# DeltaNet's row products and their transposes on 128 rows instead of 6, x loaded in two parts around the first weights, and new hand-written orders on all engines

## The chip, the cores and the metric

The kernel runs on one core of a Trainium2 chip. The metric is device time in microseconds (us); the kernel before was timed at a median of 1327.37 us over three runs (1327.2 to 1327.58). Engines are named as in the profile: PE (TensorE matmuls), PEld (its weight loads), DVE (VectorE), ACT (ScalarE), POOL (GpSimd), SP (the queue that issues most DMAs).

## The reference

A trunk of two layers over 512 tokens of width 1024. Layer 0 mixes tokens by a gated DeltaNet in both directions (8 heads of 128), layer 1 by gated linear attention (GLA, 4 heads); each is followed by a squared-ReLU MLP of width 4096, with a LayerNorm after every residual. Cut to what the change touches:

```python
proj = jnp.matmul(h, w_in).astype(F32)
qkv = jax.nn.silu(_depthwise_conv(proj[..., :A_CONV_CH], conv_w.astype(F32)))
beta = sigmoid(ba[:, :, 0]); g = -exp(a_log) * softplus(ba[:, :, 1] + dt_bias)
# per direction and head, chunks of 64 tokens:
gc = jnp.cumsum(g, axis=-1)
decay_mat = jnp.exp(jnp.where(causal, gc[..., :, None] - gc[..., None, :], -jnp.inf))
a_mat = jnp.where(strict, einsum(kb, k) * decay_mat, 0.0)
sol = triangular_solve(a_mat + I, [v * beta, kb * exp(gc)])
# then the scan over chunks with qk * decay_mat, q * exp(gc), k * exp(gc_last - gc)
```

## The kernel before

Tokens stand in four tiles of 128 (x0 to x3). The program has four stages: DeltaNet (about 0 to 400 us), MLP, GLA, MLP. Products in float32 are split into a high and a low half (`wh`, `wl` of the weights, `xth`, `xtl` of the activations), and each product is three matmuls (lines 145, 147, 148: high by high, low by high, high by low). ACT makes the high halves (line 116 for weights, 219 for x), DVE the low ones (lines 117 and 220).

**The head.** `load_x` issues four DMAs for x0 to x3, each 512 KB. PE starts with `idle` matmuls (line 824) on a zeroed tile `pz`, whose result nobody reads, and then transposes each x tile, 8 blocks of 128x128 (line 207, `tp`), with `idle` matmuls between. ACT and DVE split the transposed blocks. `load_x` returns the last such split on ACT as a mark; the weights of the gates (`bst`, split into `ws`) and the first head's key weights (`k0`) are written behind that mark. The first two products, `bap` (the gates' inputs, lines 166 and 167) and `pjk` (the keys of head 0), run in halves of 256 tokens: `bap` half 0, `pjk` half 0, `bap` half 1, `pjk` half 1.

**The gates and the first head.** From `bap`, line 1472 makes `gtp`; DVE computes the log decays in a long chain (lines 1481 to 1499, tiles `gy`, `gd`, `ge`, `gl`) and PE their sums over a chunk (`gcp`). In between stand the projections of head 0 (`pjk`, `pjq`, `pjv`, `pjz`), the convolution over time (ACT line 1612 the middle tap, DVE line 1616 four more), and Silu (lines 1643 and 1647, with a table load ahead). PE then transposes keys and queries (`ktp`, line 1664).

**The row products.** In `rows`, DVE writes a row factor in three bfloat16 pieces for two directions, 6 columns (`rsp`, lines 1683 to 1687). PE transposes them per token tile (line 1690, `rtp`: 128x6 to 6x128, four per head), ACT copies the result (`rt`, 6x512, line 1692), and in `solve` a product of the selecting matrix `sel` (6x128) with `rt` spreads a row over all 128 partitions (line 1730, `ep`: contraction over 6 rows, 512 columns, two per head). A second matmul (line 1743, `mi` by `idb`) adds a mask into the same bank. `sel` is made on POOL at the start (lines 1426 to 1431). Behind `ep` stand the solve's float16 products (`hp`, `xp`, `lv`, `nw`) and the scan's float32 ones (`m`, `op`). Each of the 8 heads does this once.

**Order.** The order on every engine is written out by hand: `ORDER` holds, for each engine, its instructions' numbers in the order in which they are to run, and `written_order` chains them. Waits across engines are added by data. Filler on PE for the solve's waits is the projections of the next head, matmul by matmul.

Of the kernel before, what the change touches and what calls it, by code (L numbers as in the profile page):

```python
# [17 lines left out]
P = 128  # L18
# [796 lines left out]
def load_x(c, x, tags, zero):  # L815
    c.new_xt()
    c.new_x()
    for t in range(NT):
        c.dma(c.xt[t], x[t * P:(t + 1) * P, :])
    idle = c.bank([P, S], F32, name="idle", tag="pj")  # L820

    def warm(n=1):
        for _ in range(n):
            c.nc.tensor.matmul(idle, zero[:, 0, :], zero[:, 0:NT, :], start=True, stop=True)
# [523 lines left out]
class GdnConst:  # L1348
# [29 lines left out]
    def masks(self):  # L1378
# [46 lines left out]
        sf = pool.tile([6, 2, P], F32, name="self", tag="E", bufs=2)  # L1425
# [4 lines left out]
        self.sel = pool.tile([6, 2, P], BF16, name="sel", bufs=1)  # L1430
        G.tensor_copy(self.sel, sf)

    def gates(self, w_in, a_log, dt_bias, conv_w, norm_g, behind):
# [32 lines left out]
        with contextlib.nullcontext():  # L1466
            ps, self.k0 = c.proj_halves([(ws, "bap", "ch"), (k0, "pjk", "ac")], {(1, 6): taps})
# [120 lines left out]
class GdnHead:  # L1588
# [63 lines left out]
    def rows(self, done):  # L1652
# [28 lines left out]
        rs = c.small.tile([P, NT, 6], BF16, name="rsp", tag="rsp")  # L1681
# [7 lines left out]
        for n in range(NT):  # L1689
            T.transpose(rtp[:6, n, :], rs[:, n, :], g.idb)  # L1690
        self.rt = pool.tile([6, S], BF16, name="rt", tag="rt", bufs=2)
        A.copy(self.rt, rtp[:6, :, :].rearrange("p n i -> p (n i)"))
# [250 lines left out]
    def finish(self, done):  # L1943
# [32 lines left out]
        0-129 134-199 206-209 200-205 226-234 210-213 130-133 235-237 290-292 246-248 257-259 268-270 287-289 309-314  # L1976
        323-325 342-347 356-358 375-377 214-217 378-380 389-391 222 218-221 223 482-484 224 408-413 422-424 225
        441-446 463-465 532-534 238-245 485-490 249-256 491-493 260-267 494-499 478-481 271-286 500-502 537-539
        293-308 503-505 542-544 315-322 547-549 552-557 560-562 508-511 326-341 565-570 348-355 573-575 584-586
        603-605 359-374 606-608 516-519 381-388 625-630 392-407 655-660 414-421 669-671 694-696 425-440 697-699  # L1980
        708-710 447-462 727-729 466-473 522-525 730-732 741-743 526-529 474-477 535 760-762 506 536 763-765 507 512
        545 774-776 513-514 546 793-795 515 520 796-798 521 815-817 530 576-583 531 822-824 540-541 833-835 587-594
        550-551 837-839 836 595-602 558-559 870-872 875-877 563 880-882 564 571 609-624 572 631-646 672-677 647-654
        661-668 885-887 890-892 846-847 678-693 893-895 848-849 700-707 898-900 903-905 711-726 906-908 733-740
        911-913 854-857 744-759 922-924 941-943 766-773 944-946 777-792 963-965 840-843 799-814 966-968 818-821
        996-998 993-995 860-863 825-832 1007-1009 1032-1034 844 1035-1037 845 850 1046-1048 851-852 873 864 874 853
        858 865-867 859 883 1065-1067 868-869 884 1098-1100 878-879 1068-1070 1079-1081 914-921 888-889 1101-1103
        1112-1114 1131-1133 925-932 896 1134-1136 933-940 897 901 1153-1155 1160-1162 902 909 947-962 910 969-971
        1171-1174 977-992 972-975 999-1006 976 1010-1031 1175-1177 1208-1210 1038-1045 1213-1215 1244-1246 1218-1220
        1049-1064 1223-1225 1228-1230 1184-1187 1071-1078 1231-1233 1236-1238 1241-1243 1082-1097 1249-1251 1260-1262  # L1990
        1104-1111 1192-1195 1178-1181 1115-1118 1123-1130 1119-1122 1279-1284 1137-1152 1301-1303 1156-1159 1163-1166
        1304-1306 1331-1333 1167-1170 1334-1336 1182 1345-1347 1183 1188 1370-1372 1189-1190 1373-1375 1191 1198-1201
        1196 1384-1386 1211 1197 1202-1207 1212 1436-1438 1403-1405 1216-1217 1221 1439-1441 1450-1452 1226-1227 1222
        1469-1471 1406-1408 1234-1235 1417-1419 1472-1474 1252-1259 1239 1491-1493 1263-1270 1240 1247 1498-1500 1509
        1271-1278 1248 1307-1314 1285-1300 1348-1353 1315-1330 1513-1515 1546-1548 1337-1344 1551-1553 1556-1558
        1510-1512 1354-1369 1561-1563 1566-1571 1376-1383 1574-1576 1522-1525 1387-1402 1579-1581 1409-1416 1582-1584
        1587-1589 1420-1435 1598-1600 1530-1533 1442-1449 1617-1619 1453-1468 1620-1622 1516-1519 1475-1490 1639-1641
        1494-1497 1501-1504 1642-1644 1669-1671 1505-1508 1672-1674 1520 1683-1685 1521 1526 1708-1710 1527-1528
        1711-1713 1529 1534 1536-1539 1722-1724 1535 1544 1549-1550 1540-1543 1545 1554 1559 1741-1743 1560 1744-1746
        1755-1757 1774-1776 1555 1564 1777-1779 1590-1597 1565 1572 1788-1790 1601-1608 1573 1807-1809 1609-1616  # L2000
        1577-1578 1810-1812 1829-1831 1585 1623-1638 1586 1645-1668 1686-1691 1847-1850 1675-1682 1836-1838 1851-1853
        1884-1886 1692-1699 1889-1891 1894-1896 1700-1707 1714-1721 1899-1901 1904-1909 1725-1740 1912-1914 1860-1863
        1747-1754 1917-1922 1758-1773 1925-1927 1780-1787 1854-1857 1868-1871 1791-1806 1936-1938 1813-1820 1955-1957
        1821-1828 1832-1835 1958-1960 1977-1979 1839-1846 1980-1982 2007-2009 1858-1859 2010-2012 2021-2023 1864-1865
        2046-2048 1866-1867 1874-1877 2049-2051 1872 1887 1873 1878-1881 1888 1882-1883 1897 2060-2062 1892-1893 1898
        2079-2081 1902-1903 2082-2084 2093-2095 1928-1935 1910 2185-2187 1939-1946 1911 2112-2114 1915 1947-1954 1916
        2115-2117 2126-2128 2145-2147 1923 2188 1961-1976 1924 1983-1987 1991-2006 1988-1990 2024-2025 2013-2020
        2026-2028 2148-2150 2030-2037 2029 2222-2224 2038-2045 2052-2059 2167-2169 2227-2229 2063-2070 2174-2176
        2189-2191 2071-2078 2085-2092 2232-2234 2237-2239 2242-2244 2096-2111 2245-2247 2192-2195 2118-2125 2250-2252
        2198-2200 2129-2144 2201 2255-2260 2151-2166 2263-2265 2170-2173 2206-2208 2177-2180 2209 2274-2276 2293-2295  # L2010
        2181-2184 2296-2298 2196 2315-2317 2197 2348-2350 2202 2318-2320 2203-2204 2345-2347 2212-2215 2205 2210
        2359-2361 2384-2386 2211 2220 2225 2216-2219 2221 2226 2230 2235 2387-2389 2231 2236 2398-2400 2240-2241
        2450-2452 2417-2422 2266-2273 2248 2523-2526 2277-2284 2249 2253 2431-2433 2254 2285-2292 2261 2453-2455
# [284 lines left out]
```

## Time and profile before

| | |
|---|---|
| median of 3 runs | 1327.37 us |
| the profiled execution's own time | 1325.86 us |
| its span, first to last instruction | 1323.8 us |
| PE busy | 1307.9 us (99%) |
| DVE busy | 1137.1 us (86%) |
| ACT busy | 773.8 us (58%) |
| POOL busy | 120.3 us (9%) |
| share of PE in the chain that ended last | 91% |

The profile shows one execution. A row of a timeline gives the start in us, the duration, the engine, the line, the operation with out<-in, partitions x elements, and in brackets the idle time before it and what ended it. Matmuls overlap one another, so what a matmul costs is read from start to start of the next, not from its duration; `128*128` ahead of a matmul's size is the rows and columns of the array that its weights take. The last row of PE starts at 1315.8 us; behind it stand the last LayerNorm and the store.

### The profile page before, as it was taken

The numbers are of one execution on the slowest core, as the hardware profiler recorded it, in microseconds if no ns is written. First come the engines' busy times: TensorE is split into PE (matmuls) and PEld (weight loads), VectorE is DVE, ScalarE is ACT, GpSimd is POOL, SyncE is SP. The second block draws the span as 40 slices with busy tenths as digits, with TensorE's granted clock in tenths as the row PEclk, the third lists the DMA queues.
The fourth block names the chain that finished last, engine by engine and source line by source line (L and its number), as shares of the span: only waits on it lengthen the run. The fifth ranks groups of instructions, "written<-read, shape, count | busy, mean of one in ns | idle before, by whom it ended". The sixth has DMA issues, their size and how long they took to land.

```text
span 1323.8 us, 22196 instructions
## 1 busy us (share of the span) xinstructions
PE 1307.9 (99%) x8726; PEld 1131.5 (85%) x8726; DVE 1137.1 (86%) x1738; ACT 773.8 (58%) x1477; POOL 120.3 (9%) x180
## 2 busy tenths in 40 slices
PE   9999999999999999999999999999999999999997
PEld 7778887888888899989888888888889899898986
DVE  6788898999868888988985999988878898989876
ACT  4666657766634556656563367757466556565640
POOL 6610000000001010000100111120000000101000
PEclk9999999999999999999999999999999999999999
DMA  7321112110334455555641486464125754738321
GB/s 197 81 64 49 48 41 58 49 49 1 113 96 118 135 152 146 164 130 176 128 126 38 123 221 150 105 143 143 57 61 166 179 128 152 149 114 203 115 64 63
DMA packets 155287, 148.84 MB, mean 112 GB/s; under 512 B 7425, under 2 KB 124193, under 8 KB 155184
## 3 DMA queue, kind: packets, MB, share of 16 engines
q1 hardware_dynamic: 144416, 115.62, 29.0%
q0 software_dynamic: 10624, 31.55, 12.6%
q8 instruction: 68, 1.11, 0.3%
q14 instruction: 35, 0.29, 0.1%
q10 hardware_dynamic: 144, 0.26, 0.1%
HBM read 118.06 MB, written 4.19 MB: 92 GB/s over the span
## 4 chain that ended last, share of the span: by engine, by line
PE 91%; ACT 4%; DVE 3%; issue 1%; DMA 1%; DVEq 0%; ACTq 0%
PE pq L145 6%; PE pq L148 6%; PE pq L147 6%; PE pX L147 3%; PE pX L148 3%; PE pX L145 3%; PE pjv L145 3%; PE pjv L148 3%; PE pjv L147 3%; PE pj L147 2%; PE pj L145 2%; PE pj L148 2%; PE pl L147 2%; PE pl L145 2%; PE pl L148 2%; PE op L1938 2%
## 5 line engine op out<-in xcount | busy, mean ns | idle before, releaser
L116 ACT CAST wh<-wst 128x1024 fp32r<-128x1024 f32 (+1 forms) x175 | 172.6, 989 | 113.3 <-DVE wst L497 28.5
L117 DVE TENSOR_TENSOR wl<-wst,wh 128x1024 fp32r<-128x1024 f32 (+1 forms) x175 | 201.0, 1152 | 37.3 <-ACT wh L116 36.7
L145 PE MATMUL pq<-xth,wh 128*128 128x256 f32 x384 | 108.3, 282 | 2.0 <-DVE h L564 1.2
L148 PE MATMUL pq<-xth,wl 128*128 128x256 f32 x384 | 108.3, 282 | 0.0
L147 PE MATMUL pq<-xtl,wh 128*128 128x256 f32 x384 | 108.2, 282 | 0.0
L117 DVE TENSOR_TENSOR w2l<-w2r,w2h 128x1024 fp32r<-128x1024 f32 x84 | 102.3, 1220 | 5.5 <-ACT w2h L116 5.2
L116 ACT CAST w2h<-w2r 128x1024 fp32r<-128x1024 f32 x84 | 87.8, 1050 | 31.8 <-issue 8.3
L148 PE MATMUL pq<-t,wl 128*128 128x256 f32 x288 | 81.1, 282 | 0.0
L147 PE MATMUL pq<-t,wh 128*128 128x256 f32 x288 | 81.0, 281 | 0.0
L145 PE MATMUL pq<-t,wh 128*128 128x256 f32 x288 | 81.0, 281 | 0.0
L145 PEld LDWEIGHTS pq<-xth,wh 128*128 128x128 f32 x384 | 72.7, 189 | 7.4 <-ACT h L568 1.7
L147 PEld LDWEIGHTS pq<-xtl,wh 128*128 128x128 f32 x384 | 72.9, 190 | 4.8
L147 PE MATMUL pX<-w2l,ah 128*128 128x512 f32 x192 | 75.5, 393 | 0.0
L148 PE MATMUL pX<-w2h,al 128*128 128x512 f32 x192 | 75.4, 393 | 0.0
L145 PE MATMUL pX<-w2h,ah 128*128 128x512 f32 x192 | 75.2, 392 | 0.0
L148 PEld LDWEIGHTS pq<-xth,wl 128*128 128x128 f32 x384 | 72.9, 190 | 0.0
L612 POOL DMA_DIRECT2D w2r<-w2r x36 | 31.0, 893 | 427.3 <-DVE w2l L117 143.0
L497 DVE TENSOR_TENSOR wst<-wst 128x512 f32<-128x512 f32 x96 | 65.4, 687 | 3.6 <-DMA wst<-in_mlp_w 2.4
L116 ACT CAST ah<-h 128x1024 fp32r<-128x1024 f32 x42 | 44.1, 1050 | 24.5 <-PE pX L147 15.4
L117 DVE TENSOR_TENSOR al<-h,ah 128x1024 fp32r<-128x1024 f32 x42 | 51.3, 1220 | 6.1 <-ACT ah L116 5.9
L145 PEld LDWEIGHTS pq<-t,wh 128*128 128x128 f32 x288 | 54.3, 189 | 2.5
L147 PEld LDWEIGHTS pq<-t,wh 128*128 128x128 f32 x288 | 54.3, 189 | 2.5
(557 smaller groups left out, 4067.2 us busy)
## 6 DMA issues: line engine op xcount, KB each, us to landing
wst<-in_mlp_w SPq DMA_DIRECT2D x64, 512.0 KB, 5.0
w2r<-in_mlp_w SPq DMA_DIRECT2D x64, 512.0 KB, 5.3
w2r<-w2r POOLq DMA_DIRECT2D x36, 512.0 KB, 5.3
wst<-in_a_w_in SPq DMA_DIRECT2D x32, 512.0 KB, 4.0
wst<-in_b_w_in SPq DMA_DIRECT2D x24, 256.0 KB, 3.6
wst<-in_a_w_out SPq DMA_DIRECT2D x8, 512.0 KB, 4.0
wst<-in_b_w_in SPq DMA_DIRECT2D x8, 512.0 KB, 5.5
ch<-wst POOLq DMA_DIRECT2D x8, 512.0 KB, 5.9
```

The source lines that it names most:

```text
L116: nc.scalar.copy(hi, src)
L117: self.low = nc.vector.tensor_tensor(lo, src, hi.bitcast(F32), ALU.subtract)
L145: mm(ps, ah, bh, start=start, stop=False, **kw)
L147: mm(ps, ah, bl, start=False, stop=False, **kw)
L148: mm(ps, al, bh, start=False, stop=stop, **kw)
L497: V.tensor_tensor(a, a, b, ALU.add)
L612: nc.gpsimd.dma_start(a, b, accum_op=ALU.add)
L1938: T.matmul(op[:, n, :], l, r, start=i == 0, stop=i == len(mm) - 1)
```

## The change

Four things are edited.

1. **128 rows.** `sel` is a 128x2x128 tile, zero outside its 6 rows, and `rt` is 128x512. `rsp` is one of two standing tiles of 128x4x128 that POOL fills with zeros once; DVE writes the 6 columns as before. So the transposes take 128 columns, the copy 128 partitions, and the product `ep` contracts over 128 rows, 122 of them zero.
2. **The mark.** `load_x` returns the split of x1 instead of that of x3, so that the first weights may be issued, and their products placed, ahead of x2 and x3.
3. **Banks.** `bap` and `pjk` of the head take banks of the pool `pj` instead of `ch` and `ac`, which the transposes of x use.
4. **Orders.** The numbers of all five engines are other ones, in DeltaNet, in parts of the MLPs and in GLA.

```diff
@@ load_x
-    return c.marks[-1]
+    return c.marks[1]
@@ GdnConst.masks
-        sf = pool.tile([6, 2, P], F32, name="self", tag="E", bufs=2)
+        sf = pool.tile([P, 2, P], F32, name="self", tag="E", bufs=2)
...
-        self.sel = pool.tile([6, 2, P], BF16, name="sel", bufs=1)
+        self.sel = pool.tile([P, 2, P], BF16, name="sel", bufs=1)
         G.tensor_copy(self.sel, sf)
+        self.rs = [pool.tile([P, NT, P], BF16, name=f"rsp{i}", bufs=1) for i in range(2)]
+        for t in self.rs:
+            G.memset(t, 0.0)
@@ GdnConst.gates
-            ps, self.k0 = c.proj_halves([(ws, "bap", "ch"), (k0, "pjk", "ac")], {(1, 6): taps})
+            ps, self.k0 = c.proj_halves([(ws, "bap", "pj"), (k0, "pjk", "pj")], {(1, 6): taps})
@@ GdnHead.rows
-        rs = c.small.tile([P, NT, 6], BF16, name="rsp", tag="rsp")
+        rs = g.rs[h % 2]
...
-            T.transpose(rtp[:6, n, :], rs[:, n, :], g.idb)
-        self.rt = pool.tile([6, S], BF16, name="rt", tag="rt", bufs=2)
-        A.copy(self.rt, rtp[:6, :, :].rearrange("p n i -> p (n i)"))
+            T.transpose(rtp[:, n, :], rs[:, n, :], g.idb)
+        self.rt = pool.tile([P, S], BF16, name="rt", tag="rt", bufs=2)
+        A.copy(self.rt, rtp.rearrange("p n i -> p (n i)"))
@@ ORDER
     "PE": """
-        0-129 134-199 206-209 200-205 226-234 210-213 130-133 235-237 290-292 246-248 257-259 268-270 287-289 309-314
...
```

What moves in the order is shown at three places; line numbers behind the edits are 3 higher after the change.

The first is DVE at the very start, before the change and then after it; `pz_95` is the zeroed tile that the `idle` matmuls read.

```order
L1521 MEMSET pz_95 128x512
L1521 MEMSET pz_97 128x512
L1521 MEMSET pz_99 128x512
L1521 MEMSET pz_101 128x512
L1521 MEMSET pz_103 128x512
L1444 COPY two<-ident 32x32
```

```order
L1524 MEMSET pz_101 128x512
L1524 MEMSET pz_99 128x512
L1524 MEMSET pz_103 128x512
L1447 COPY two<-ident 32x32
L1524 MEMSET pz_95 128x512
L1524 MEMSET pz_97 128x512
```

The tile that PE's first matmuls wait for is now zeroed fourth, behind three others and a copy.

The second is PE in the head: a piece of the difference, from the first half of `bap` on (`xt_107` and `xt_108` are x2 and x3, `pjk` the keys of head 0).

```order
 L166 MATMUL bap<-xth,ws 64x256
 L167 MATMUL bap<-xtl,ws 32x256
+L207 MATMUL tp<-ident,xt_107 128x128 x4
+L824 LDWEIGHTS pz_95
+L824 MATMUL idle<-pz_95 128x512
+L207 MATMUL tp<-ident,xt_107 128x128 x4
+L824 LDWEIGHTS pz_95
+L824 MATMUL idle<-pz_95 128x512
+L207 MATMUL tp<-ident,xt_108 128x128 x8
 L145 MATMUL pjk<-xth,wh 128x256
 L147 MATMUL pjk<-xtl,wh 128x256
```

The 16 transposes of x2 and x3, which stood ahead of `bap`, stand between its first half and the first half of `pjk`, with two `idle` matmuls; ahead of `bap` now stand 8 `idle`, x0's 8 transposes, one `idle`, x1's 8, and two `idle`. On the SP queue the order is x0, x1, `bst`, the weights of `pjk`, x2, x3, where it was x0 to x3, `bst`, the weights.

The third is DVE in the chain from `gtp` to the queries' convolution of head 0 (`pjq`), before the change and then after it; `wl` is the low half of a later weight tile.

```order
L1616 SCALAR_TENSOR_TENSOR sil<-pjk,cw,sil 128x510
L1495 SCALAR_TENSOR_TENSOR gl<-gl,gd 128x128
L117 TENSOR_TENSOR wl<-wst,wh 128x1024
L1495 SCALAR_TENSOR_TENSOR gl<-gl,gd 128x128
L1616 SCALAR_TENSOR_TENSOR sil<-pjq,cw,sil 128x510
L1495 SCALAR_TENSOR_TENSOR gl<-gl,gd 128x128
L1616 SCALAR_TENSOR_TENSOR sil<-pjq,cw,sil 128x511
```

```order
L1619 SCALAR_TENSOR_TENSOR sil<-pjk,cw,sil 128x510
L1496 TENSOR_SCALAR gl<-gd 128x128
L1498 SCALAR_TENSOR_TENSOR gl<-gl,gd 128x128 x3
L1619 SCALAR_TENSOR_TENSOR sil<-pjq,cw,sil 128x510
L1498 SCALAR_TENSOR_TENSOR gl<-gl,gd 128x128
L1619 SCALAR_TENSOR_TENSOR sil<-pjq,cw,sil 128x511
```

One weight split has left this chain, and one more step of the gates stands ahead of the queries' last tap (six `gl` steps of line 1498, five before). On PE, the number of projection matmuls between the last one of `pjq` and the first `ktp` is 30, where it was 42 (24 of `pjv` and 18 of `pjz`); between that `ktp` and the transposes `rtp` it is 45, where it was 54.

More of the change, by code (lines that the diff above doesn't have):

```diff
@@ new lines @@
+        441-443 293-300 444-446 463-465 301-308 315-322 485-490 326-341 491-499 348-355 500-505 532-534 537-539
+        542-544 547-549 568-569 508-511 359-374 552-557 381-388 560-562 565-567 570 516-519 392-407 573-575 584-586
+        414-421 603-608 625-630 655-660 425-440 522-525 669-671 447-462 694-696 466-473 697-699 708-710 727-729
+        474-477 535 506 526-529 507 512 536 730-732 741-743 545 513-514 546 760-765 515 520 774-776 793-798 576-583
+        521 530 815-817 822-824 531 540 833-835 587-594 541 550 837-839 836 595-602 551 558 870-872 875-877 559 563
@@ new lines @@
+        609-624 564 880-882 571 639-654 572 631-638 661-668 672-677 846-847 678-693 885-887 848-849 700-707 890-892
+        906-908 711-726 893-895 911-913 733-740 898-900 854-857 744-759 903-905 922-924 941-943 766-773 944-946
+        963-965 777-792 966-968 993-995 799-806 860-863 807-814 840-843 818-821 825-828 996-998 1007-1009 1032-1034
+        844 829-832 873 1035-1037 1046-1048 845 850 864-866 874 851-852 867 883 1065-1070 853 858 884 1079-1081
+        1098-1103 1112-1114 859 914-921 868 1131-1133 869 878 1171-1174 925-932 879 888 1134-1136 933-940 889 896
@@ new lines @@
+        7939-7941 7906-7911 7954-7959 7978-7980 7960-7962 7966-7968 7963-7965 7981-7983 8014-8016 7969-7971 7984-7989
+        7972-7974 8017-8022 7975-7977 8002-8007 7990-7992 8008-8013 8023-8025 8062-8064 8026-8028 8134-8136 8029-8031
+        8137-8148 8032-8034 8149-8157 8035-8037 8086-8088 8038-8040 7993-7995 8041-8043 8089-8091 7996-7998 8158-8160
+        8065-8067 7999-8001 8044-8046 8161-8163 8047-8061 8092-8094 8068-8073 8095-8097 8074-8076 8098-8100 8077-8085
+        8101-8133 8164-8181
@@ new lines @@
+        475 474 489 484 477 480 485 478-479 481 490-491 537 486 492 487 476 493 549 494-495 502 496-497 533 506 503
+        498 507 499 534 508 500 509 501 510-511 565 512 535 514 536 513 504 515 505 545 516 518 605 519 523 546
+        524-526 517 547 538 527 529 521 530 539 531 528 540-541 553 532 548 559 542 606 543-544 560 550 561 566
+        551-552 567 562 568 554 607 555-556 558 569-570 563-564 579 557 571-576 583 591 589 584 590 577 592 585 578
+        586 580 587-588 522 581-582 613 620 595 593 597 596 599 594 600 602 601 608 603 612 609-610 598 614 611 604
@@ new lines @@
+        323-327 368 312-313 330-331 317 332-333 338 341 360 318 340 319 321 339 320 322 342 344 328-329 345 365
+        346-349 334 350 335-337 351-353 406 356 358 357 359 367 355 354 362 364 363 369-371 377 372-373 424 374
+        378-380 429 386-387 375 388 376 389-390 393-396 423 381 401 431 382 384 383 385 402 391-392 485 404 428 397
+        399 398 403 400 405 407-416 419 421 420 422 417 430 440 418 425 486 427 426 432-437 487 441-442 449-452
+        438-439 453 444 456-459 443 464 445 467 447 446 448 454 465 455 466 468-469 460 462 461 463 470-478 481 483
```

487 lines of the change are left out of this document (233 added, 254 removed).

## The prediction

> **What bounds the kernel now.** I read the stages first (busy time of each engine in stretches of the span), then PE's timeline around the matmuls that the change widens, then the chain of waits in the first 15 us.
>
> ```profile
> 60.00:350.00 290.00, 288.41 (x2589) 238.03 (x2589) 261.01 (x521) 191.22 (x510) 9.41 (x21) 1.00 0.19 54
> ```
>
> The columns are the stretch, its length, then busy time and instructions of PE, PEld, DVE, ACT, POOL. In DeltaNet PE is busy for 288.4 of 290 us, DVE for 261.0 (90%). So there is no idle time to win there; what can be won is matmuls that take longer from start to start than they must. The timeline shows such ones at line 1730 (`ep` from `sel`, 6 rows):
>
> ```profile
> 56.85 0.39 PE L1730 MATMUL ep<-rt,sel 6*128 6x512 bf16 x1
> 57.17 0.50 PE L145 MATMUL pjz<-xth,wh 128*128 128x512 f32 x1
> 57.51 0.40 PE L147 MATMUL pjz<-xtl,wh 128*128 128x512 f32 x1
> 57.75 0.40 PE L148 MATMUL pjz<-xth,wl 128*128 128x512 f32 x1
> 57.98 0.39 PE L1743 MATMUL ep<-mi,idb 128*128 128x512 bf16 x1
> 58.03 0.58 PE L145 MATMUL pjv<-xth,wh 128*128 128x512 f32 x1
> 58.44 0.40 PE L147 MATMUL pjv<-xtl,wh 128*128 128x512 f32 x1
> ```
>
> A split-float matmul of 512 columns takes 0.23 us from start to start (57.75 to 57.98). The 6-row product and the one behind it take 0.66 (56.85 to 57.51). Its twin, the mask product of the same shape on 128 rows, and the two around it take 0.69 for three (57.75 to 58.44), so the twin costs 0.23. The 6-row product thus loses 0.66 - 0.46 = 0.20 on leaving. On entering it loses 0.10, which the next piece shows; that piece has the transposes `rtp` too.
>
> ```profile
> 222.58 0.39 PE L1901 MATMUL m<-r,xf 128*128 128x128 f32 x2
> 222.89 0.39 PE L1690 MATMUL rtp<-idb,rsp 128*6 128x128 bf16 x4
> 223.21 0.50 PE L145 MATMUL pjv<-xth,wh 128*128 128x512 f32 x1
> 223.55 0.40 PE L147 MATMUL pjv<-xtl,wh 128*128 128x512 f32 x1
> ...
> 224.23 0.39 PE L1916 MATMUL m<-vd,kt 128*128 128x128 f32 x2
> 224.55 0.60 PE L1730 MATMUL ep<-rt,sel 6*128 6x512 bf16 x2
> 225.08 1.16 PE L1718 MATMUL kk<-sil 128*128 128x128 f32 x8
> ```
>
> A float32 block of 128 columns takes 0.11 (`ktp` in the next fence, four in 0.44). 224.23 to 224.55 is 0.32 for two of them, 0.10 too long. So one entry and exit cost 0.30. For `rtp`, 222.58 to 223.55 is 0.97, where two blocks (0.22), four transposes at 0.056 (0.22) and one wide matmul (0.23) make 0.67: 0.30 lost per group of four. What 128-column transposes of 2-byte numbers cost stands here:
>
> ```profile
> 67.62 0.60 PE L1863 MATMUL ktp<-ident,sil 128*128 128x128 f32 x4
> 68.06 0.61 PE L1773 MATMUL xp<-idh,Dd 128*128 128x128 f16 x8
> 68.51 0.40 PE L1801 MATMUL lv<-Dd,ath 128*128 128x64 f16 x8
> 68.74 0.48 PE L145 MATMUL pjz<-xth,wh 128*128 128x512 f32 x1
> 69.06 0.39 PE L147 MATMUL pjz<-xtl,wh 128*128 128x512 f32 x1
> ```
>
> Eight take 0.45 (0.056 each), nothing is lost on entering, and on leaving for a split-float matmul 0.09 (0.32 instead of 0.23).
>
> **The change part by part.** *128 rows.*
>
> ```profile
> L1730 PE MATMUL ep<-rt,sel x16: 374/385/385, 55.4 to 348.6; 6*128 6x512 bf16 x16
> ```
>
> There are 16 products (count, shortest, median and longest in ns, then first and last start); one pair (224.55) stands together, so 15 entries and exits at 0.30 go away: -4.5 us. The 8 groups of transposes keep an exit of 0.09 and lose 0.21: -1.7. Together -6.2 us, all on PE, which sets the end. For the products this is sure to within some 0.3, since the twin differs in its rows alone. For the transposes there is a row that speaks against it:
>
> ```profile
> 12.73 0.28 PE L167 MATMUL bap<-xtl,ws 128*32 128x256 f32 x1
> 12.85 0.28 PE L166 MATMUL bap<-xth,ws 128*64 128x256 f32 x1
> ```
>
> These alternate between 32 and 64 columns of the array at 0.12 us each with no loss, so few columns alone need not cost; the bound for the transposes is 0 to -1.7, and I take -1.7, since the group itself shows the loss. The Trainium skill, page TensorEngine Tiling (Array Packing), section Key Properties, says that a change of tiling mode drains the engine, and its modes go by rows and by columns; by that rule both sums go away, but `bap` should drain at each step as well, and the trace shows that it does not.
>
> The other engines see the same work: ACT's copy of 6x512 takes as long as one of 128x512, DVE writes the same 6 columns. POOL gets two fills of 128x512 and its selection steps now stand behind a fill that waits for ACT's copy of the keys. From that copy (41.4 us before) I count some 6 us of POOL work to `sel`, 47 to 48, first read at about 52: it is hidden with 4 us to spare, and each us beyond would be lost at the first `ep`.
>
> *The head.*
>
> ```profile
> 0.98 2.65 DVE L1521 MEMSET pz<- 128x512 uint32 x5 [0.98 <-PEq L2287]
> ```
>
> ```profile
> 1.52 3.17 PE idle L824 x7
> 4.69 0.85 PE tp L207 x4
> 5.54 0.43 PE idle L824
> ...
> 8.08 0.44 PE tp L207 x4
> 8.52 0.21 PE idle L824
> ...
> 10.61 1.07 ACT xth L219 x2
> 11.69 0.31 ACT ws L159
> 12.02 0.44 DVE ws L160
> 12.46 0.14 issue
> ```
>
> Now the chain to the first half of `pjk`. It starts 2.09 us behind `bap` at 12.59, thus at about 14.5 before, with all 32 transposes done (16 `bap` matmuls at 0.12). After: each fill is 0.54, so three fills, the copy (about 0.2) and `pz_95` put the first `idle` matmul 1.85 later, at 3.37. Eight at 0.43 end at 6.8; x0's eight transposes at the early rate (0.85 per four) 8.5; one `idle` 8.9; x1's eight 9.8 to 10.6, say 10.1 with the last result out; then one split on ACT (0.55), `ws` on ACT 0.31 and on DVE 0.44, issue 0.14: `bap` at about 11.6. Half of it (1.9), 16 transposes (1.76) and two `idle` (0.42) give `pjk` at 15.7, which is 1.2 later. PE's transposes run at half rate until some moment between 6.8 and 8.1 (0.85, then 0.44 per four), about 7.4; were that moment fixed in time, the same chain gives 15.0, 0.5 later. Below, x could come out of this up to 1.6 earlier only if `bap` did not wait at all; the late start excludes it. Bounds +0.5 to +1.3; I take +0.9. The Trainium skill, page TensorE: Matmul & The Clock Gate, Part 1, gives 3.4 us of activity in a free-running window until the full rate; by that rule the moment lies between 6.8 and 10.2, and my estimate by it is +0.1 to +1.3.
>
> *The first `ktp`.*
>
> ```profile
> 36.53 1.28 ACT L1643 ACT_TABLE_LOAD   x1 [1.19 <-DVE sil L1616]
> 37.82 1.06 ACT L1643 ACTIVATE sil<-sil 128x1024 f32<-128x1024 f32 x1
> 38.94 0.66 PE L1664 MATMUL ktp<-ident,sil 128*128 128x128 f32 x4 [0.39 <-ACT sil L1643]
> 53.54 0.39 PE L1690 MATMUL rtp<-idb,rsp 128*6 128x128 bf16 x4 [0.26 <-DVE rsp L1687]
> ```
>
> PE already waits 0.39 here, and DVE has no idle time from `gtp` to the last tap. After the change PE comes 12 matmuls, 2.8 us, earlier (30 instead of 42), while DVE's chain loses one weight split (1.2) and gains one `gl` step (0.3): 0.9 shorter. That leaves 1.9 more of waiting. Steps of this chain were stretched by POOL's masks, which now run earlier, by up to 1.1. Bounds -0.4 (no wait left) to +1.9; I take +1.0. What queues behind `ktp` is `gcp` and the projections.
>
> *The first `rtp`.* Its filler shrinks by 9 matmuls, 2.1 us. Its chain (Silu of v and z, logarithm, the six small steps on DVE) loses a weight split on ACT and a convolution tap among DVE's steps, but the copy of the z projection comes later. Bounds -0.3 and +2.1; I take +0.8, nearer the low end, as the chain shrinks too.
>
> *The orders elsewhere.* The solve's products are followed by other kinds 124 times instead of 129; at 0.09 each, -0.4. Waits of PE on other engines behind 60 us stand in nine rows that sum to 4.2 us, this one ahead:
>
> ```profile
> PE pq L145 <- DVE h L564: 1.2, 1, 1.2
> ```
>
> It lies in an MLP. A new order may win or lose some 2 us of these, and I take 0.
>
> Sum: -6.2 + 0.9 + 1.0 + 0.8 - 0.4 = -3.9 us. The profiled execution took 1325.86 us (span 1323.8), 1.5 below the median; on its own time that is 1322.0, on the median of 1327.37 it is 1323.5.
>
> **The rivals.** *The start loses nothing* (the waits at `ktp` and `rtp` are filled, POOL disturbs DVE less, the rate rises early): 1327.4 - 6.2 - 0.4 = 1320.8. For it: waits at both places were under 0.4 before. Against: the late first matmul, and filler that shrinks more than its chain.
>
> *The padding takes nothing away*, because the loss comes with the bf16 tile that ACT has just written, or the kinds around it, rather than with rows: -0.4 + 2.7 = 1329.7, slower than before; up to 1331.5 with the upper bounds. It decides if `ep` on 128 rows still takes 0.66 with the matmul behind it. For it: the columns of `bap`. Against: the twin, which is bf16 too, into the same bank.
>
> *DVE takes PE's place.* DeltaNet's 290 us lose 5.5; DVE's 261 then fill 92%, in a chain with PE. If half of the gain returns as short waits on DVE: about 1326.5. Against it: PE waited for DVE there under 1 us in all, at 90%.
>
> **How the numbers follow.** Forecast 0.52, the start loses nothing 0.27, DVE in PE's place 0.13, padding takes nothing 0.08. A measurement of this kernel can tell about 0.2%, 2.7 us. The forecast's own range is 1321.5 to 1325.7; three quarters of it lie below 1324.7. So faster 0.39 + 0.27 + 0.02 = 0.68; slower 0.05 (the upper part of the third rival's 0.08, little else); no change 0.27. The range reaches down to the second case with 2 us of new orders, 1319, and up to 1327.5.
>
> **What would show it.** In the profile after: (a) `ep` from `sel` reads 128*128 and the matmul behind it starts as behind the mask product; (b) PE's first matmul near 3.4 us and the first `pjk` near 15.4 instead of 14.5; (c) waits of 1 to 2 us at the first `ktp` and near 1 at the first `rtp`; (d) from 60 to 350 us no new waits. The prediction is wrong if (a) fails, if the early waits stay under 0.5, or if waits on DVE grow past 2 us behind 60.

## The result, and the profile after

The changed kernel takes 1316.63 us (median; 1316.31 to 1317.22) where the kernel before takes 1327.47 on the same chip: ratio 0.9919, 95% interval 0.9901 to 0.9936. A second comparison on one chip gave 1316.82 against 1325.95, ratio 0.9929 (0.9917 to 0.9942). So it is some 9 to 11 us faster. The forecast was 3.9 us faster (1323.5, range 1319.0 to 1327.5): the sign was right, the size was not.

The part of the page with busy times, and the stretch of DeltaNet from the view of stages (same columns as in the prediction), of the changed kernel:

```profile
PE 1295.9 (99%) x8724; PEld 1129.0 (86%) x8726; DVE 1133.9 (86%) x1738; ACT 771.9 (59%) x1477; POOL 118.6 (9%) x182
```

```profile
60.00:350.00 290.00, 287.31 (x2619) 244.03 (x2619) 263.01 (x526) 193.26 (x519) 6.29 (x14) 1.00 0.19 54
```

PE still fills the span. In the 290 us it now gets 2619 matmuls through instead of 2589: PE was idle for only 1.6 us of it before, so the gain is matmuls that follow each other sooner. PE's timeline around the first `rtp` and the first `ep` from `sel` of the changed kernel:

```profile
51.27 0.38 PE L1693 MATMUL rtp<-idb,rsp 128*128 128x128 bf16 x4 [1.18 <-DVE rsp L1690]
51.47 0.48 PE L145 MATMUL pjq<-xth,wh 128*128 128x512 f32 x1
51.78 0.40 PE L147 MATMUL pjq<-xtl,wh 128*128 128x512 f32 x1
...
52.70 0.40 PE L148 MATMUL pjq<-xth,wl 128*128 128x512 f32 x1
52.94 0.39 PE L1733 MATMUL ep<-rt,sel 128*128 128x512 bf16 x1
53.17 1.05 PE L1721 MATMUL kk<-sil 128*128 128x128 f32 x8
```

`ep` is entered after 0.24 and left after 0.23, with nothing lost on either side. The four transposes and the wide matmul behind them take 0.51 (51.27 to 51.78).

To see where the 9 us lie I follow single products that both kernels have, from one to the next. The first `pjk` (row quoted from each timeline, before and after):

```profile
14.48 0.28 PE L145 MATMUL pjk<-xth,wh 128*128 128x256 f32 x1
```

```profile
14.70 0.36 PE L145 MATMUL pjk<-xth,wh 128*128 128x256 f32 x1
```

Then the products `pq<-xth,wh`, 192 in each MLP, from the view of one tile (count, shortest, median and longest in ns, first and last start in us): first and second MLP of the kernel before, then of the changed one.

```profile
L145 PE MATMUL pq<-xth,wh x192: 277/282/384, 461.1 to 699.8; 128*128 128x256 f32 x192
...
L145 PE MATMUL pq<-xth,wh x192: 277/283/357, 1034.4 to 1264.0; 128*128 128x256 f32 x192
```

```profile
L145 PE MATMUL pq<-xth,wh x192: 274/282/385, 455.4 to 692.0; 128*128 128x256 f32 x192
...
L145 PE MATMUL pq<-xth,wh x192: 277/282/283, 1026.9 to 1255.4; 128*128 128x256 f32 x192
```

| stretch | before | after | difference | forecast |
|---|---|---|---|---|
| head, to the first `pjk` | 14.5 | 14.7 | +0.2 | +0.9 |
| DeltaNet, first `pjk` to first `pq` | 446.6 | 440.7 | -5.9 | -4.8 |
| first MLP, first to last `pq<-xth` | 238.7 | 236.6 | -2.1 | 0 |
| to the first `pq` of the second MLP (GLA) | 334.6 | 334.9 | +0.3 | 0 |
| second MLP, first to last `pq<-xth` | 229.6 | 228.5 | -1.1 | 0 |

The rest, to the last matmul, is the same. These sum to -8.6; the spans differ by 8.7 (1323.8 and 1315.1). The first MLP is the surprise: PE's order is the same there, product by product, and so is the work. The second MLP's 1.1 is one wait, which stands in the view of PE's waits of the kernel before and is missing after it (the row `PE pq L145 <- DVE h L564: 1.2, 1, 1.2` of the prediction). The longest waits of the changed kernel in that view:

```profile
PE idle L824 <- DVE pz L1524: 3.4, 1, 3.4
PE ktp L1667 <- ACT sil L1650: 2.1, 4, 0.8
PE pjv L147 <- DVE wl L117: 1.3, 2, 0.7
PE rtp L1693 <- DVE rsp L1690: 1.2, 1, 1.2
```

The waits at the later `ktp` have grown, from this row of the kernel before:

```profile
PE ktp L1664 <- ACT sil L1647: 0.6, 1, 0.6
```

Behind 60 us PE's waits sum to 4.7 us (4.2 before): the second MLP's is gone, those at `ktp` have grown by 1.5, and two at `pjv` of GLA (on `wl`, 1.3) have come.

### The profile page after: what moved, and what is told of

The parts are those of the page before. It is cut to its first block, busy times and chain, and to the rows that moved or that the text cites. A ratio compares the mean times of both kernels' runs of the same rounds, so it can differ in the third digit from the quotient of the medians.

```text
span 1315.1 us, 22214 instructions
## 1 busy us (share of the span) xinstructions
PE 1295.9 (99%) x8724; PEld 1129.0 (86%) x8726; DVE 1133.9 (86%) x1738; ACT 771.9 (59%) x1477; POOL 118.6 (9%) x182
## 4 chain that ended last, share of the span: by engine, by line
PE 92%; ACT 4%; DVE 3%; DMA 1%; issue 1%; DVEq 0%; ACTq 0%; POOLq 0%
PE pq L145 6%; PE pq L147 6%; PE pq L148 6%; PE pX L145 3%; PE pX L148 3%; PE pX L147 3%; PE pjv L145 3%; PE pjv L147 3%; PE pjv L148 3%; PE pj L145 2%; PE pj L147 2%; PE pj L148 2%; PE pl L145 2%; PE pl L147 2%; PE pl L148 2%; PE scp L1224 2%
## 5 line engine op out<-in xcount | busy, mean ns | idle before, releaser
L145 PE MATMUL pq<-xth,wh 128*128 128x256 f32 x384 | 107.8, 281 | 0.8 <-ACT h L555 0.8
L145 PE MATMUL pq<-t,wh 128*128 128x256 f32 x288 | 80.5, 280 | 0.0
L145 PEld LDWEIGHTS pq<-xth,wh 128*128 128x128 f32 x384 | 72.7, 189 | 5.8 <-ACT h L555 1.0
L145 PE MATMUL pX<-w2h,ah 128*128 128x512 f32 x192 | 75.5, 393 | 0.0
L145 PEld LDWEIGHTS pq<-t,wh 128*128 128x128 f32 x288 | 54.2, 188 | 2.2
```

The source lines that it names most:

```text
L145: mm(ps, ah, bh, start=start, stop=False, **kw)
```

## The experiments

The runs are numbered in the order in which they ran. In the differences `-` is the changed kernel (in the third and twelfth run the kernel before), `+` the run. Distances between products come from each run's trace; places of tiles are addresses in bytes within a partition, as the build gave them out. `pz64` of the expectations is `pz_95`, the tile that the `idle` matmuls read.

### What the width is worth: the first two runs and the twelfth

```
-            T.transpose(rtp[:, n, :], rs[:, n, :], g.idb)
+            T.transpose(rtp[:6, n, :], rs[:, n, :6], g.idb)
-        A.copy(self.rt, rtp.rearrange("p n i -> p (n i)"))
+        A.copy(self.rt[:6, :], rtp[:6, :, :].rearrange("p n i -> p (n i)"))
-            T.matmul(ps, g.sel[:, d, :], self.rt, start=True, stop=True)
+            T.matmul(ps, g.sel[:6, d, :], self.rt[:6, :], start=True, stop=True)
```

> The changed kernel with its products and transposes narrow again: ep reads 6 rows of sel and rt, rtp writes 6 columns; tiles, fills and all orders stay as changed. My theory (a narrow product or group costs an entry and an exit, 0.30 and 0.21 us, all on the bound engine): +6.2 us against the changed kernel, 1322.8 us, about 1.004 times faster than the kernel before, and the start-to-start of ep and the matmul behind it back from 0.46 to 0.66. If only the products cost: +4.5. Rival (the padding takes nothing away, the gain lies in the orders and places): within 1 us of the changed kernel, 1316.6.

The second run has the last pair of lines alone.

> The changed kernel with only the ep products narrow again (6 rows of sel and rt); the rtp transposes stay 128 wide. My theory: +4.5 us against the changed kernel, 1321.1 us, and the narrow transposes of the first run are worth the 1.7 between the two. Rival (the column count of the transposes costs nothing): this run takes as long as the first, 1322.8 by the one price or more. Rival (padding takes nothing): 1316.6.

Measured: 1322.21 (ratio to the kernel before 0.9969, 95% interval 0.9957 to 0.9981) and 1320.22 (0.9954, 0.9942 to 0.9967). Against the changed kernel's 0.9929 that is +5.3 and +3.3 us. The traces are sharper, from the first `pjk` to the first `pq`: 446.3 (15.6 to 461.9) and 444.4 (14.9 to 459.3), against 440.7. So the width is worth 5.6 us in this order: 3.7 in the products, 1.9 in the transposes. PE's timeline of the second run at the same place as above:

```profile
52.88 0.39 PE L148 MATMUL pjq<-xth,wl 128*128 128x512 f32 x1
53.20 0.38 PE L1733 MATMUL ep<-rt,sel 6*128 6x512 bf16 x1
53.51 1.16 PE L1721 MATMUL kk<-sil 128*128 128x128 f32 x8
54.60 0.39 PE L1733 MATMUL ep<-rt,sel 6*128 6x512 bf16 x1
54.92 0.39 PE L1746 MATMUL ep<-mi,idb 128*128 128x512 bf16 x1
```

The entry costs 0.32 instead of 0.24. The exit into the square blocks `kk` costs 0.31 instead of 0.23, and the exit into the bf16 twin 0.32; the prediction's exit into a split-float wide product cost 0.20 more than it should. So an exit costs 0.1 or 0.2, by what follows, and the products come to 0.18 to 0.30 each.

The twelfth run puts the width alone into the kernel before:

```
-        self.sel = pool.tile([6, 2, P], BF16, name="sel", bufs=1)
+        self.sel = pool.tile([P, 2, P], BF16, name="sel", bufs=1)
+        self.rs = [pool.tile([P, NT, P], BF16, name=f"rsp{i}", bufs=1) for i in range(2)]
+        for t in self.rs:
+            G.memset(t, 0.0)
     (rtp, rt and ep as in the changed kernel; all orders, the start and its banks as before)
```

> The kernel before with its own orders, start and banks, and the 128 row products, transposes and fills alone (the two new fills stand behind sel in POOL's order). The tiles lie as in the changed kernel. By the runs so far: 5.1 us for the width and 2.5 us for the places less than the kernel before: 7.6, ratio 0.9943. My forecast's price of the width (6.2): 8.7 less. If the new orders were needed to turn the width into time, or POOL's two fills come late at the first ep: less than 5 us. What then separates this run from the changed kernel (9.1 less than before) is the orders' own part: 1 to 2 us net, with the late start of PE counted against them.

Measured: 1317.70, ratio 0.9930 (0.9918 to 0.9943), as fast as the changed kernel within what can be told. That is 9.3 us less than the kernel before by the ratio: more than the 7.6 that I expected, nearer to the 8.7 by the prediction's price. From the first `pjk` to the first `pq` it takes 440.5, 6.1 less than the kernel before (446.6) and as long as the changed one:

```profile
14.42 0.28 PE L145 MATMUL pjk<-xth,wh 128*128 128x256 f32 x1
...
L145 PE MATMUL pq<-xth,wh x192: 274/282/386, 454.9 to 691.5; 128*128 128x256 f32 x192
```

So in DeltaNet the new orders gain nothing on balance, and the width gains all of it. By the spans (1315.8, and 1314.9 of the changed kernel's second profiled execution) everything else in the change is worth 0.9, one execution each.

### The first MLP: the third, sixth, ninth to eleventh, thirteenth and fourteenth run

Three small `rsp` tiles (64 bytes each) left the pool that lives through the whole program, when `rsp` moved into DeltaNet's own pool. Every tile allocated behind them, all those of the MLPs among them, lies 192 bytes lower after the change. The third run does this alone, in the kernel before:

```
-        rs = c.small.tile([P, NT, 6], BF16, name="rsp", tag="rsp")
+        rs = self.pool.tile([P, NT, 6], BF16, name="rsp", tag="rsp", bufs=3)
```

> The kernel before, its work and orders untouched, with the three small rsp tiles (64 bytes each) allocated in DeltaNet's own pool instead of the pool that lives through the whole program. So every tile of the first MLP lies 192 bytes lower, as in the changed kernel. Theory of places (the products pq<-t of the first MLP went from 119.4 to 115.7 ns from start to start because t now begins at a multiple of 128 bytes, 64 off before): pq<-t near 116 ns between 400 and 730 us, 2 us less than the kernel before, 1325.4. Rival (it is another order of loads or of DVE and ACT, or another chip): pq<-t stays at 119 to 120, and the time at 1327.4.

Measured: 1323.73, ratio 0.9979 (0.9971 to 0.9988), so 2.8 us faster with no other change. DeltaNet gains nothing from it: 447.0 from the first `pjk` to the first `pq` (446.6 before). Its first MLP takes 236.6 (461.1 to 697.7), like the changed kernel's:

```profile
L145 PE MATMUL pq<-xth,wh x192: 274/282/386, 461.1 to 697.7; 128*128 128x256 f32 x192
```

How the gain looks in the timeline shows best in one stretch of 24 products `pq<-t` that stand together in the first MLP: first and last of them, before, then after.

```profile
521.94 0.29 PE L145 MATMUL pq<-t,wh 128*128 128x256 f32 x1
...
524.70 0.29 PE L148 MATMUL pq<-t,wl 128*128 128x256 f32 x1
```

```profile
515.86 0.28 PE L145 MATMUL pq<-t,wh 128*128 128x256 f32 x1
...
518.48 0.28 PE L148 MATMUL pq<-t,wl 128*128 128x256 f32 x1
```

23 steps take 2.76 and 2.62: 120 and 114 ns. My first idea was that `t` gains when it begins at a multiple of 128 bytes. The sixth run put x and `t` of both MLPs there:

```
+        c.const.tile([P, 16], F32, name="pad0", bufs=1)
+        c.small.tile([P, 8], F32, name="pad1", bufs=1)
+            gp.tile([P, 8], F32, name="pad2", bufs=1)
```

> The changed kernel with three unused pads (64, 32 and 32 bytes), so that xth, xtl, all tiles of both MLPs and so t in both MLPs begin at a multiple of 128 bytes; work and orders untouched. Before: xth and xtl 64 off, t of the second MLP 32 off. If the place of the moving operand is what counts: pq<-xth and pq<-xtl go from 118 to 119 ns to about 116 in both MLPs (some 1150 products, 3 us) and t of the second MLP from 118.3 to about 116 (some 400, 1 us): 4 us less than the changed kernel. If the 512 wide products from xth (227 ns) gain 6 too, several us more in DeltaNet. Rival (t gained by something else that moved with it, such as the tiles DVE and ACT write): xth stays at 118 to 119, and the time within 1 us of the changed kernel.

Measured: 1316.66 (0.9926, 0.9913 to 0.9940), as the changed kernel, but the first MLP was slow again, 238.4 (455.0 to 693.4), and `xth` no faster (118.5 ns). The idea fell. That the time did not rise with the first MLP has its reason further on: the stretch to the second MLP took 332.2 instead of 334.9, and products of 512 columns were faster there, `oa<-wh,oth` 228.0 ns from start to start instead of 231.6. So the times of these runs mix gains and losses of places in several stages. The next two runs tried a best place for `t` alone, and for `x` too; both stand on the run with `pz64` zeroed first, below (its time is 1314.93).

```
+        c.small.tile([P, 56], F32, name="pad1", bufs=1)
+            gp.tile([P, 8], F32, name="pad2", bufs=1)
```

> The run with pz64 zeroed first, with two unused pads (224 and 32 bytes), so that t begins at 128 beyond a multiple of 256 in both MLPs (so far in the first only; in the second 160 beyond). The places seen so far, bytes beyond a multiple of 256 and ns from start to start of pq<-t: 0: 119.4 (both MLPs), 64: 119.5, 96: 117.8, 128: 115.8, 160: 118.3. If the place of t within 256 bytes sets it: 118.3 to 116 in the second MLP, 1 us less than that run, 1313.9. Rival (the place counts only together with that of wh or of other tiles): the second MLP stays at 118.

```
+        c.const.tile([P, 48], F32, name="pad0", bufs=1)
+        c.small.tile([P, 8], F32, name="pad1", bufs=1)
+            gp.tile([P, 8], F32, name="pad2", bufs=1)
```

> As the run with t at 128 in both MLPs, with xth, xtl, wh and wl moved by 192 bytes, so that these too begin at 128 beyond a multiple of 256 (192 before; 0 in the aligned run). If the place of any moving operand counts: pq<-xth and pq<-xtl go from 118.5 to 116, some 1150 products, 3 us less than with t alone, 1311. Rival (it is t alone, read in rows of 1024 bytes, while x is read in pieces of rows of 2048): xth stays at 118 to 119, the time within 0.5 of the run with t alone. If t goes back to 119 here, the place of wh counts too.

```
+        c.small.tile([P, 16], F32, name="pad1", bufs=1)
```

> The run with pz64 zeroed first, with one unused pad of 64 bytes: t begins 192 beyond a multiple of 256 in the first MLP and 224 beyond in the second. Nothing else moves against x and wh. If 128 is a best place and the cost grows with the distance from it: 119 to 120 ns in the first, about 119 in the second, 2 us more than the run without the pad, 1317. Rival (no law of that kind): anything between 115 and 120.

Measured: 1314.20 (0.9905, 0.9889 to 0.9920), 1315.62 (0.9914, 0.9900 to 0.9927) and 1315.44 (0.9912, 0.9898 to 0.9926). The times tell little apart; the traces do. With `t` at 128 in both MLPs the second MLP's `pq<-t` went from 118.3 to 116.7 ns. But in the tenth run, with `t` at the same place and `xth` and `wh` moved, both MLPs were slow, 119.4 to 119.5, as was the first MLP of the eleventh. The same stretch of 24 in the tenth run:

```profile
514.78 0.28 PE L145 MATMUL pq<-t,wh 128*128 128x256 f32 x1
...
517.53 0.28 PE L148 MATMUL pq<-t,wl 128*128 128x256 f32 x1
```

That is 120 ns again. What orders all the values is how far `t` lies from its weights `wh`, counted within 128 bytes (mean of all steps between neighbouring `pq<-t`, worked out from the traces):

| `t` less `wh`, within 128 bytes | ns from start to start | seen in |
|---|---|---|
| 0 | 119.4 to 119.6 | kernel before, 1st MLP; sixth and tenth run, both; eleventh, 1st |
| 32 | 117.4 to 117.7 | kernel before, 2nd; eleventh, 2nd |
| 96 | 118.3 | changed kernel, 2nd |
| 64 | 115.9 to 116.7 | changed kernel, 1st; ninth run, both |

`xth` and `wh` had been at distance 0 in every run. The thirteenth run puts 64 bytes between them and leaves `t` at 64 from `wh`; the fourteenth puts 64 bytes between the weights `ah`, `al` and the moving tiles `w2h`, `w2l` of the second layer.

Both add to the ninth run, the second of them to the first:

```
+        c.wst.tile([P, 16], F32, name="pad3", bufs=1)
```

> The run with t at 128 in both MLPs, with one more unused pad of 64 bytes between the tiles of x and those of the weights: xth and xtl stay, wh, wl and all that lies behind (t too) move by 64. So far t was slow (119.4) where t and wh began at the same place within 128 bytes (t/wh beyond a multiple of 256: 64/192, 0/0, 192/192, 128/128), fast (115.8 to 116.4) at 128/192, between at 96/192, 160/192 and 224/192 (117.8, 118.3, 117.5); xth and wh were at the same place in every run. If the distance of moving tile and weights within 128 bytes is what counts, 64 best: t stays fast at 192/0, and xth and xtl go from 118.5 to about 116 (1150 products, 3 us): 1311, and perhaps more in the 512 wide products of DeltaNet and GLA that read xth. Rival (the place of t alone, or of x alone): t goes back to 119.4 at 192, as in the run where it lay there, and xth stays: 1316.

```
+            pool.tile([P, 16], F32, name="pad4", bufs=1)
```

> As the run before this one, with 64 more bytes ahead of w2h and w2l in both MLPs, so that these, which the 512 wide products of the second layer read as moving tiles, lie 64 off ah and al, their weights (0 off in every run so far). If the distance counts for 512 wide products too: pX and pY go from 229 to 232 ns to about 226 (some 860 products, 3 to 4 us less). Rival (512 wide products have no such cost): they stay at 229 to 232, and the time within 0.7 us of the run before.

Measured: 1310.72 (0.9881, 0.9865 to 0.9898) and 1310.09 (0.9878, 0.9863 to 0.9893). The thirteenth run's forecast of 1311 by the distance held; its rival said 1316. All 256 wide products gain: `pq<-xth` and `pq<-xtl` run at 114.3 to 115.8 ns instead of 118 to 119, and the 24 at 113 to 114:

```profile
514.48 0.28 PE L145 MATMUL pq<-t,wh 128*128 128x256 f32 x1
...
517.09 0.28 PE L148 MATMUL pq<-t,wl 128*128 128x256 f32 x1
```

```profile
L145 PE MATMUL pq<-xth,wh x192: 276/276/386, 454.9 to 689.1; 128*128 128x256 f32 x192
```

The first MLP takes 234.2 instead of 238.7 before the change. The 512 wide products do not follow this law: those from `xth` in DeltaNet got slower, from 229 to 230 ns to 233, and DeltaNet 1.4 us longer (12.6 to 454.9, against 12.6 to 453.5 in the ninth run). In the fourteenth run's first MLP `pX<-w2h,ah` and `pX<-w2l,ah` gained 3 ns and `pX<-w2h,al` lost 4; its time is 0.6 less, as the rival said, within the interval of the thirteenth. So 64 bytes of distance gain where 256 columns move. Products of 512 columns move with the places too, by 3 to 4 ns up or down, by no law that these runs show. These two runs are the fastest versions, some 6 us below the changed kernel; 1.9 of that comes from the start that they share with the seventh run.

### The head and the early waits: the seventh and the eighth run

The seventh run changes one thing in DVE's order: the tile on which PE's idle matmuls wait is zeroed first; it had been the fifth instruction, behind three fills and a copy.

```
 DVE:
-        3 2 4 17 0 1 ...
+        0 3 2 4 17 1 ...
```

> The changed kernel with one change of DVE's order: pz64, on which PE's idle matmuls wait, is zeroed first instead of fifth, so that PE starts at about 1.5 instead of 3.4 us. My theory of the head (the late first matmul delays the full rate): the idle matmuls end 1.9 earlier, bap starts when ws is there, and the head gains 0.3 to 1.2 us, 0.7 in the mean. Rival (the first weights and not PE set bap, or the full rate comes at a moment of its own): pjk at 14.4 to 14.7 as in the changed kernel, within 0.3.

Measured: 1314.93 (0.9915, 0.9901 to 0.9929), 1.9 us less than the changed kernel on the same chip: more than the 0.3 to 1.2 that I expected. PE's timeline of the head, of the changed kernel:

```profile
3.43 3.59 PE L824 MATMUL idle<-pz 128*128 128x512 f16 x8 [3.43 <-DVE pz L1524]
6.81 1.32 PE L207 MATMUL tp<-ident,xt 128*128 128x128 f32 x8
...
10.71 0.33 PE L166 MATMUL bap<-xth,ws 128*64 128x256 f32 x1 [1.06 <-DVE ws L160]
```

and of the run:

```profile
1.53 3.60 PE L824 MATMUL idle<-pz 128*128 128x512 f16 x8 [1.53 <-DVE pz L1524]
4.92 1.49 PE L207 MATMUL tp<-ident,xt 128*128 128x128 f32 x8
...
8.99 0.33 PE L166 MATMUL bap<-xth,ws 128*64 128x256 f32 x1 [1.06 <-DVE ws L160]
...
13.23 0.36 PE L145 MATMUL pjk<-xth,wh 128*128 128x256 f32 x1
```

The whole chain moves with the first matmul. One trace says little of the size, since the full rate comes at another moment in each execution: in the six with the late zeroing, the trace's record of the granted clock begins, at full rate, 2.9 to 5.9 us behind the first matmul, and for each us that it comes later the first `pjk` starts half a us later. Over all traces with this head the first `pjk` starts at 14.91 in the mean where `pz64` is zeroed late (six executions, 14.16 to 15.64) and at 12.99 where it is zeroed first (six, 12.54 to 13.79); with the head of the kernel before it starts at 14.32 (four, 14.10 to 14.48). So two tiles of x and then the first weights gain 1.3 us, and the late zeroing costs 1.9 of them back.

The eighth run gives the changed kernel the start of the kernel before, up to the first two `ep`:

```
-    proj_halves([(ws, "bap", "pj"), (k0, "pjk", "pj")], ...)
+    proj_halves([(ws, "bap", "ch"), (k0, "pjk", "ac")], ...)
     PE, DVE, ACT and the loads: the order of before up to about 55 us, the changed one behind it
```

> The changed kernel (wide products, its orders from about 55 us on) with the start of the kernel before: PE's order up to the first two ep, DVE's up to the last step of the first rsp, ACT's up to the second exponent, the loads of the first weights, and the banks of bap and pjk as they were. My theory (less filler ahead of the first ktp and rtp costs 1.8 us of waiting, the late start of PE 0.3 to 1.2): some 2 us faster than the changed kernel. Rival (the old start's own surplus comes back at the seam, or the fillers only move the wait): within 0.7 us of it.

Measured: 1319.18 (0.9946, 0.9933 to 0.9958), 2.4 us more than the changed kernel, where I had expected 2 less. The early waits do go: the first `rtp` waits 0.24 instead of 1.18. Right behind it come others, at the seam of the two orders:

```profile
53.68 0.38 PE L1693 MATMUL rtp<-idb,rsp 128*128 128x128 bf16 x4 [0.24 <-DVE rsp L1690]
57.53 0.38 PE L1746 MATMUL ep<-mi,idb 128*128 128x512 bf16 x1 [0.47 <-ACT qd L1735]
59.29 0.25 PE L1763 MATMUL hp<-icc,a 128*128 128x4 f16 x4 [0.68 <-DVE a L1750]
60.49 0.27 PE L1763 MATMUL hp<-icc,a 128*128 128x4 f16 x4 [0.95 <-DVE a L1750]
61.19 0.38 PE L1763 MATMUL hp<-dc,a 128*128 128x4 f16 x8 [0.43 <-DVE dc L1765]
```

The four behind it sum to 2.5 us: work used as filler early is missing a few us later. But there is more in this trace. From 60.0 to 66.8 us the granted clock is one half, and products of 512 columns stand 0.42 us apart instead of 0.23 (the first row is from the view of stretches, its columns as in the prediction, then the granted clock, the DMA share and GB/s):

```profile
60.00:66.70 6.70, 5.78 (x47) 4.73 (x47) 4.61 (x9) 2.26 (x4) 4.98 (x11) 0.50 0.11 13
...
63.15 0.63 PE L147 MATMUL pjv<-xtl,wh 128*128 128x512 f32 x1
63.57 0.63 PE L148 MATMUL pjv<-xth,wl 128*128 128x512 f32 x1
```

At half rate 6.8 us do the work of 3.4 at most, so this stretch can hold all of the 2.4. The other executions point the same way: four of the five have a mean granted clock of 0.995 or 0.996 and take 1318.58 to 1320.86, the fifth has 0.999 and takes 1316.84, as the changed kernel (1316.82, all at 0.999). So my 2 us failed in any case, and in the one execution with the full clock the rival held: the old start neither gained nor lost. That the waits at the seam set off the half rate is likely by their place (the last one before it ends at 59.29), but no run shows it. Nor does this run show what the old start is worth with orders made for it; the twelfth run is better for that.

### The orders behind the middle: the fourth run, and the changed kernel again

The fourth run is the changed kernel up to the middle of the first MLP, with the orders of before on all engines behind it.

> The changed kernel up to the middle of the first MLP; behind it the orders of all engines are those of the kernel before, so the GLA part runs as before. Counted by work done, the GLA part of the changed kernel starts 1.8 us worse (first 50 us) and ends 0.8 better than before. If the new GLA orders carry a part of the gain that I had put at 0: +0.8 us against the changed kernel, 1317.4. Rival (they carry none; the difference is chance of one execution): 1316.6 within 0.4. Rival (they carry the rest of what I missed): +2.5 or more, 1319.

Measured: 1318.64 (0.9943, 0.9930 to 0.9955), 1.9 us more than the changed kernel by the ratios, between the 0.8 that I expected and the rival's 2.5. In the trace the second MLP takes 1.2 longer (229.7), and its wait is back in the view of waits:

```profile
PE pq L145 <- DVE h L564: 1.0, 1, 1.0
```

The stretch with GLA takes 335.8, 0.9 longer; but with the old orders throughout, in the twelfth run, it takes 334.8, as the changed kernel's 334.9. So that part comes with the seam, and the new orders of GLA itself gain nothing.

The changed kernel itself ran once more beside the runs on the head:

> The changed kernel unchanged, on the same chip and against the same runs of the kernel before as the next three. By the traces it should be 8.7 us faster than the kernel before (the spans), by the first medians 10.8. Of the first us I expect that they differ between executions: the moment at which PE reaches its full rate cost the four profiled executions with the late first matmul between 0.25 and 1.24 us against the kernel before, at one and the same program.

Measured: 1316.82 (0.9929, 0.9917 to 0.9942), 9.1 us less than the kernel before: nearer to the spans than to the first medians.

## Why the prediction was right or wrong

The trace moved by -8.6 where the sum said -3.9. What lies between: -2.1 in the first MLP and -1.1 in the second, where the sum had 0; -1.7 more than forecast from the new order in DeltaNet; -0.7 in the head; +0.6 for the width; +0.3 on the way to the second MLP.

- **128 rows, -6.2.** Right: 5.6 us in the new order, 6.1 in the old. Of the parts, the products were put too high (4.5; measured 3.7) and the transposes about right (1.7; 1.9). The products' 0.30 joined the entry of one with the exit of another that ran into a wide product; of the narrow `ep` in the trace of before, 10 of 15 run into square blocks, where the exit costs 0.1. The rule of the Trainium skill (TensorEngine Tiling (Array Packing), Key Properties) that a change of mode drains the engine agrees with both, but gives no price, and `bap` still alternates at 0.12 without one.
- **The head, +0.9.** Right in sign, with a bound that the single trace missed (+0.2 against the one of before, by means +0.6). That the moment of the full rate decides was right; it moves from execution to execution, and I had set it from one. The 2.09 us from `bap` to `pjk` that I read there is 1.89 (12.59 to 14.48); the sum itself goes by 1.9.
- **The first `ktp`, +1.0: the wait lies elsewhere.** No wait at the first `ktp` is left in the view. PE waits 0.8 earlier, at the first `pjz`, and the row names DVE's last tap on `pjk`, which ends 0.15 before:

```profile
29.87 0.74 DVE L1619 SCALAR_TENSOR_TENSOR sil<-pjk,cw,sil 128x510 f32<-128x510 f32 x1
...
30.75 0.47 PE L145 MATMUL pjz<-xth,wh 128*128 128x512 f32 x1 [0.79 <-DVE sil L1619]
```

  The third edit and the new order together make PE wait there. With `pjk` of the head in the pool `pj`, the first `pjz` gets the same bank, as the build gives banks out, and must leave it to DVE until that tap has read it; and the new order brings `pjz` to this point 16 us behind the first `pjk`, where it was 20. In the kernel before, `pjk` lay in a bank of another pool, and no `pjz` waited. The sum had no term for the change of banks; the size came out near by chance.
- **The first `rtp`, +0.8.** Measured 1.18 where there was 0.26: right, within its bounds.
- **Fewer exits of the solve's products, -0.4: mis-sized.** Too narrow a count. From 60 to 435 us of the span PE's next matmul differs in rows, columns or type from the one ahead of it 537 times before and 482 times after; I had counted the 5 of one kind. With the width the same (the first run against the kernel before) PE's time over that of the same matmuls back to back fell by 2.1 us in that stretch, about what the waits of the start had cost, and this although the waits of over 0.15 us in it rose from 1.5 to 2.5. The third run, with the places alone, shows none of it. So it comes from the new order; that the fewer changes of kind are what does it is argued from the count, not shown by a run.
- **The rest of the program, "I take 0": the step that failed.** The sum had no term at all for tiles that move: -2.1 in the first MLP, where no instruction of PE had changed its place, shown by the third run. And a new order was worth more than a row of waits tells. As a sum the waits behind 60 us did stay (4.2 before, 4.7 after), but the one that I quoted, `pq` at line 145 with 1.2, went and took 1.1 out of the second MLP, while those that came in its place did not show in the time: the 1.5 more at `ktp` in DeltaNet were paid for by matmuls that follow each other sooner, and what paid for the 1.3 at `pjv`, in a stretch that grew by 0.3, is open. The +-2 that I allowed for new orders did not cover all this together. Of the signs, (a) held and (d) failed with the new waits at `ktp`; (b) held for PE's first matmul, (c) for the first `rtp`. None of the three signs of being wrong came, as none of them looks at the MLPs.
- **POOL, hidden.** Right: no wait on `sel` shows.
- **The rivals.** "The start loses nothing" gave 1320.8 and did not happen: the start lost some 2 us by 60 us. "The padding takes nothing away" fell with the first run (its upper end, given as 1331.5, comes to 1332.3 by the upper bounds +1.3, +1.9 and +2.1 and the -0.4). "DVE takes PE's place" did not happen, PE's waits on DVE behind 60 us stay near 2 us in all.

## What to carry to other kernels

Price a matmul with few rows by what stands ahead of it and behind it, since its entry and exit depend on the neighbours; padding with zeros to 128 rows is free where the engines around it see the same sizes. A diff that moves a tile from one pool to another moves every tile behind it, and can change the speed of code that it does not touch: compare such stretches product by product before giving the gain to the visible change. When a product moves to another bank, ask which tile takes that bank next, and which engine must have read it by then. And where PE is left with short waits close together, look at the granted clock of that stretch before giving the loss to the waits.

## What the runs showed of the hardware that was not expected

- **Distance of moving tile and weights.** Split-float products with 256 columns start every 118 to 120 ns where the moving tile and its weights begin at the same place within 128 bytes, and every 114 to 117 where they are 64 apart; those from `t`, 119.5 at 0, stand in between at 32 and 96. In the first MLP that makes 234.2 us of 238.7. Why it is so is not settled; products of 512 columns follow another law, which these runs don't settle either: those from `xth` lost 3 to 4 ns. The Trainium skill, page SBUF — State Buffer, section "SBUF: two separate sides", says that on the engines' side only the port pair that VectorE and GpSimd share makes anyone wait, and calls PE's read port for weights a second, independent one. Nothing here speaks against the first, which is between engines; against the second stands the pace measured by distance, which shows that the places of PE's two operands count together.
- **The full rate comes at another moment each time.** With the same program up to there, the eight transposes behind the idle matmuls take 1.32 us (above) or 1.91:

```profile
6.82 1.91 PE L207 MATMUL tp<-ident,xt 128*128 128x128 f32 x8
```

  (first run). Over all 16 traces the record of the granted clock begins 2.9 to 6.0 us behind PE's first matmul, and the steps before it are twice as long; the views of stretches read 1.00 ahead of it too, where they have no record. The Trainium skill, page TensorE: Matmul & The Clock Gate, Part 1, tells of a window of 3.4 us that runs freely; as an estimate from it the full rate would come after 3.4 to 6.8. Thirteen traces agree; three, at 2.9, 3.0 and 3.35, do not.
- **The rate can fall again in the middle.** In the eighth run the granted clock went back to one half for 6.8 us, at 60 us of the span, behind no wait of PE longer than 0.7 us in the 10 us ahead.
